# Retention layer: the values of two heads as seven products of halves, and the order of the layer's units rewritten

## The chip, the cores and the metric

The kernel runs on one core of one Trainium2 chip. A core has a matrix engine (TensorE; PE in the profile, with its weight loads as PEld), a vector engine (VectorE, DVE), an activation engine (ScalarE, ACT), a general engine (GpSimd, POOL) and a queue engine (SyncE, SP) that only issues transfers. Each engine carries out its own instructions strictly in the order in which the program issued them; engines wait for each other by semaphores. The metric is the device time of one execution in microseconds, the median over the runs shown. Times in rows of the trace are microseconds from the first instruction of the profiled execution.

## The reference

A trunk of two layers over 512 tokens of width 1024, all in float32. Layer 0 mixes tokens with a gated MLP, layer 1 with retention; each is followed by a squared-ReLU MLP (1024 to 4096 to 1024), and a last RMSNorm ends the trunk. The change lies in the retention layer:

```python
h = rmsnorm(x, norm_mix_g[1])
proj = h @ w_in                              # 1024 x 6144
q, k, v, g = split(proj, [1024, 2048, 4096]) # 4 heads: q, k 256 wide; v, g 512 wide
q, k = rotary(q), rotary(k)
for each head:                               # decay[i, j] = gamma ** (i - j) for i >= j
    o = ((q @ k.T) * decay) @ v
    o = rmsnorm(o, head_norm_g)              # over the 512 columns of the head
y = o * silu(g)
x = x + y @ w_out                            # 2048 x 1024
```

(The reference runs over chunks of 128 tokens with a state; over the 512 tokens of this input that is the formula above.)

## The kernel before

Everything is feature-major: `xT` holds the residual as 8 tiles of 128 features by 512 tokens. A float32 product is done as three fast products: each operand is split in a high part (a rounded copy, by ScalarE) and a low part (what the rounding left, by VectorE), and `mm3` (L263) issues high*high, high*low and low*high into one PSUM bank. So weights arrive in 1 MB blocks (`Raw`, 512 columns of a 512-row or 256 columns of a 1024-row slab), each is cut in two pieces of 128 x 1024 numbers (`Piece`), and each piece is split by one ScalarE copy (L222, tile wH) and one VectorE subtraction (L229, tile wL). A piece normally feeds 24 matmuls of 512 columns.

The program order is written out by hand. `step` records a unit of work with its pieces; a loop at the end (L1129) issues the units one after the other. A unit issues its matmuls and then, in this order, `advance()` (the next part of every unfinished evacuation), `refill()` and its hook `behind` (other work placed there). `refill` (L248) runs ahead: it issues the high part of the piece three units on and the low part of the piece two units on; after each low part `load_raws` (L185) issues every further weight load for which a place is free: two own buffers, a third (`extra`) where a stage has set one up, or a tile of the common pool of 16 8-KB buffers (`big`). A weight block that is the sum of two blocks of the matrix is loaded by SP, and the second block is then added by a transfer that POOL issues (L201, `accum_op=add`); that instruction waits on POOL until the first load has landed.

The second MLP matrix already runs through `seven` (L724): the 2x2 block product [activations: token halves by feature halves] x [weights: row halves by column halves] is formed from seven products of halves instead of eight (Strassen's scheme in Winograd's form). Products 1, 3, 4 and 5 use sums of activation blocks, which `make(s)` forms on VectorE (L753 to L760) and splits in high and low parts (L768, L769), one product ahead; each product takes two weight pieces that feed only 12 matmuls each; the results are added into a token-major tile from three running PSUM accumulators (L799 copy on ScalarE the first time, L801 add on VectorE afterwards). There the products alternate with units of the first MLP matrix (`up`).

The norm is applied late. `hH`, `hL` hold x*g split in two; the factor 1/rms per token is put on the results. `norm` (L344) computes it in four parts that hooks call one by one: split the sum of squares (ScalarE, POOL); two matmuls, a masked sum on VectorE and a power on POOL (L299, tile r4); split of that and two diagonal matrices on VectorE (L336, tile dg); two matmuls that spread it over the partitions and a copy to `rbc` (L342, tile wide).

The retention layer consists of these units of four pieces each (96 matmuls): `v_unit(h)` (values; scaled with r4 and split at evacuation, L920, L921), `qk_unit(h)` (queries and keys; rotary at evacuation with tables that carry rbc: L890 to L900), `g_unit(h)` (gates: z = psum*rbc on VectorE, L996; sigmoid on ScalarE, L997; z*sigmoid on VectorE, L999) and `o_unit(h)` (output projection). `scores(h, j)` and `av(h, c)` are small groups of matmuls that run in the hooks; `head_norm(h)` and `make_y(h, ..)` finish a head. The order before is v0, qk0, g0 (with the scores of head 0), qk1 (with av 0), v1 (scores 1, norm of head 0), g1 (av 1), o0 (norm 1), and then qk, v, g, o(h-1) for heads 2 and 3, and o3.

Of the kernel before, what the change touches and what calls it, by code (L numbers as in the profile page):

```python
# [10 lines left out]
F32 = mybir.dt.float32  # L11
# [77 lines left out]
def trunk(ctx, tc, x, norm_mix_g, norm_ffn_g, a_w_in, a_b_in, a_v_norm_g, a_w_s, a_b_s, a_w_out,  # L89
# [170 lines left out]
    def do(fn):  # L260
        step(lambda: fn())
# [461 lines left out]

    def seven(l, q):  # L724

        w = mlp_w2[l]

        def part(i, j):
            r, c = 1024 * q + 512 * i, 512 * j
            return w[r : r + 512, c : c + 512].rearrange("(k p) n -> p k n", p=P)  # L730
# [9 lines left out]
        def block(h, ts, c):  # L740
            return aF[2 * q + h][:, 2 * c : 2 * c + 2, ts]

# [3 lines left out]
        def make(s):  # L746

            def src(c):
                if s in (0, 2, 6):
                    return block(*((0, lo_t), None, (1, lo_t), None, None, None, (1, hi_t))[s], c)  # L750
                if s == 1:
                    sums["s", c] = half(tmp(f"sa{l}{q}{c}", "uz"))
                    nc.vector.tensor_sub(out=sums["s", c], in0=block(0, hi_t, c), in1=block(1, hi_t, c))  # L753
                elif s == 3:
                    nc.vector.tensor_sub(out=sums["s", c], in0=sums["s", c], in1=block(0, lo_t, c))
                elif s == 4:
                    nc.vector.tensor_add(out=sums["s", c], in0=sums["s", c], in1=block(1, lo_t, c))
                else:
                    sums["d", c] = half(tmp(f"sd{l}{q}{c}", "sq"))
# [4 lines left out]
            sp = parts[s] = big([P, 2, 4, T // 2], F32R, f"sp{l}{q}{s}")  # L764
            for c in range(2):
                v = src(c)
                hi, lo = sp[:, 0, 2 * c : 2 * c + 2, :], sp[:, 1, 2 * c : 2 * c + 2, :]
                nc.scalar.copy(out=hi, in_=v)  # L768
                nc.vector.tensor_sub(out=lo, in0=v, in1=f32(hi))  # L769
# [4 lines left out]

        PLAN = (0, 1, 2, 3, 5, 4, 6) if q == 2 else range(7)

        def one(s, i):
            after = dict(zip(PLAN, PLAN[1:])).get(s)

            def run(p):  # L780
                bk = BANK[s]
                if i == 0 and s in FIRST:
                    banks[bk] = [acc(f"sm{l}{q}{bk}{t}") for t in range(2)]
                sp = parts[s]
                for t in range(2):
                    ts = slice(t * P, (t + 1) * P)
                    for k in range(2):
                        kk = 2 * i + k
                        mm3(banks[bk][t], sp[:, 0, kk, ts], sp[:, 1, kk, ts], p.hi[:, k, :], p.lo[:, k, :], s in FIRST and kk == 0, kk == 3, True)
                advance()  # L790
                refill()
                if i == 0 and after is not None:
                    make(after)
                if i == 1:
                    (m, n), op = OUT[s]
                    for t in range(2):
                        v = tok[n][:, 2 * m + t, :]
                        if (n, m) in fresh:
                            nc.scalar.activation(v, banks[bk][t], AF.Copy, scale=1.0 if op == ALU.add else -1.0)  # L799
                        else:  # L800
                            nc.vector.tensor_tensor(out=v, in0=v, in1=banks[bk][t], op=op)  # L801
                    fresh.discard((n, m))
            return run

        return (lambda: make(0)), [lambda s=s: [step(one(s, i), pl[s][i]) for i in range(2)] for s in PLAN]

    fresh = set()

    def dense(l, hooks):
# [6 lines left out]
        for q in range(3):  # L816
            pl = pieces_f(mlp_w1[l], (0, D), (1024 * (q + 1), 1024 * (q + 2)))
            first, products = seven(l, q)
            do(first)
# [51 lines left out]
    nrm1 = norm("mix1")  # L871
    tab, qk, vv, pp, oo, gt = {}, {}, {}, {}, {}, {}
    POFF = [0, 512, 896, 1152]

    def load_b():
        tab["t"] = big([P, 4, T], F32, "trg")
        nc.sync.dma_start(out=tab["t"][:, 0:2, :], in_=trig)
        tab["d"] = big([P, H, T], F32, "dec")
        nc.sync.dma_start(out=tab["d"], in_=decay)

    def trig_scaled():
        for i in range(2):
            nc.vector.tensor_mul(tab["t"][:, 2 + i, :], tab["t"][:, i, :], rbc)

    def rope(h, which, pa, pb):
        cos, sin = tab["t"][:, 2, :], tab["t"][:, 3, :]
        if which == 0:
# [37 lines left out]
    def scores(h, j):  # L925
# [10 lines left out]
        def gen():  # L936
            pm = tmp(f"pm{h}{j}", "sq")
            hi, lo = pp[h][0][:, POFF[j] : POFF[j] + n], pp[h][1][:, POFF[j] : POFF[j] + n]
            nc.vector.tensor_mul(pm[:, :n], ps[:, :n], tab["d"][:, h, :n])
            nc.scalar.copy(out=hi, in_=pm[:, :n])  # L940
# [4 lines left out]
    def av(h, c):  # L945

        if c == 0:
            oo[h] = big([P, 4, T], F32, f"o{h}")
        vhi, vlo = vv[h]
# [7 lines left out]
        def gen():  # L957
# [8 lines left out]
            nc.scalar.activation(o, ps, AF.Copy, scale=gT[:, HG + 4 * h + c : HG + 4 * h + c + 1])  # L966
            yield
# [34 lines left out]
    def v_unit(h, behind=None):  # L1002
        tokens(pieces_t(bw, (0, D), (VW + h * DV, VW + (h + 1) * DV)), hs, evac_vv(h), f"vv{h}", behind)

    def g_unit(h, behind):
        pl = pieces_f(bw, (0, D), (GWT + h * DV, GWT + (h + 1) * DV))
        for i in range(4):
            feat(pl[i], hs, evac_g(h, i), f"g{h}_{i}", behind.get(i))

# [18 lines left out]
    hn0, sc1 = head_norm(0), each(scores, 1)  # L1028
    fin = {0: nxt(hn0), 1: nxt(hn0, 2), 2: lambda: (next(hn0, None), make_y(0, (0, 1))), 3: lambda: make_y(0, (2, 3))}
# [148 lines left out]
```

## Time and profile before

| | |
|---|---|
| median of 3 runs | 1372.65 us (1372.46 to 1373.21) |
| the profiled execution's own time | 1372.68 us |
| its span, first to last instruction | 1371.0 us |
| TensorE busy | 1360.9 us, 99% of the span |
| VectorE / ScalarE / POOL busy | 856.5 us (62%) / 566.7 us (41%) / 166.5 us (12%) |
| granted TensorE clock, mean | 0.998 |
| retention layer, first to last matmul | about 625.6 to 1025.4 us |

A matmul's row lasts about 0.39 us, though one starts every 0.227 us, as they are pipelined: 24 matmuls of 512 columns take 5.44 us. So the time of TensorE is counted in starts, and a bubble is seen as a hole between two starts. For the other engines the start-to-start distance of two instructions that wait for nothing is what one costs.

### The profile page before, as it was taken

The numbers are of one execution on the slowest core, as the hardware profiler recorded it, in microseconds if no ns is written. First come the engines' busy times: TensorE is split into PE (matmuls) and PEld (weight loads), VectorE is DVE, ScalarE is ACT, GpSimd is POOL, SyncE is SP. The second block draws the span as 40 slices with busy tenths as digits, with TensorE's granted clock in tenths as the row PEclk, the third lists the DMA queues.
The fourth block names the chain that finished last, engine by engine and source line by source line (L and its number), as shares of the span: only waits on it lengthen the run. The fifth ranks groups of instructions, "written<-read, shape, count | busy, mean of one in ns | idle before, by whom it ended". The sixth has DMA issues, their size and how long they took to land.

```text
span 1371.0 us, 15352 instructions
## 1 busy us (share of the span) xinstructions
PE 1360.9 (99%) x6184; PEld 1131.5 (83%) x6184; DVE 856.5 (62%) x1088; ACT 566.7 (41%) x812; POOL 166.5 (12%) x132
## 2 busy tenths in 40 slices
PE   9999999999999999999999999999999999999997
PEld 7888888888888888888888888888888888888886
DVE  7756756675666756775655574474594665665653
ACT  4646634334544434422333432333333543444342
POOL 4001111130100000021112110100121000100002
PEclk9999999999999999999999999999999999999999
DMA  6332222245674748322222222132127375674721
GB/s 233 126 104 92 67 87 93 93 133 153 154 206 126 212 126 184 124 102 94 80 75 78 76 92 93 62 115 70 62 93 213 92 185 160 155 207 126 174 85 61
DMA packets 115799, 166.70 MB, mean 122 GB/s; under 512 B 2880, under 2 KB 67984, under 8 KB 115472
## 3 DMA queue, kind: packets, MB, share of 16 engines
q1 hardware_dynamic: 102448, 139.50, 30.5%
q0 software_dynamic: 12672, 25.17, 10.8%
q8 instruction: 48, 0.79, 0.2%
q10 hardware_dynamic: 608, 1.06, 0.2%
q14 instruction: 23, 0.19, 0.0%
HBM read 163.62 MB, written 2.10 MB: 121 GB/s over the span
## 4 chain that ended last, share of the span: by engine, by line
PE 95%; DVE 2%; DMA 1%; issue 0%; ACT 0%; POOL 0%; SPq 0%; POOLq 0%; DVEq 0%; ACTq 0%
PE up L266 24%; PE g L266 6%; PE ro L266 6%; PE vv L266 6%; PE qk L266 6%; PE u L266 6%; PE o L266 6%; PE v L266 4%; PE dt L266 3%; PE dn L266 2%; PE av L266 2%; PE sm11a L266 2%; PE sm10a L266 2%; PE sm01a L266 2%; PE sm00a L266 2%; PE sm12a L266 2%
## 5 line engine op out<-in xcount | busy, mean ns | idle before, releaser
L229 DVE TENSOR_TENSOR wL<-raw,wH 128x1024 fp32r<-128x1024 f32 x235 | 300.3, 1282 | 49.9 <-issue 13.8
L222 ACT CAST wH<-raw 128x1024 fp32r<-128x1024 f32 x235 | 243.9, 1045 | 78.6 <-PE dt L266 12.8
L266 PE MATMUL up<-hH,wH 128*128 128x512 f32 x480 | 187.2, 390 | 0.2 <-ACT xtok L1047 0.2
L266 PE MATMUL up<-hL,wH 128*128 128x512 f32 x480 | 186.8, 389 | 0.0
L266 PE MATMUL up<-hH,wL 128*128 128x512 f32 x480 | 186.8, 389 | 0.0
L701 ACT ACTIVATE aF<-r 128x512 f32<-128x512 f32 x54 | 34.2, 633 | 218.2 <-DVE r L700 218.2
L700 DVE SCALAR_TENSOR_TENSOR r<-up,wide 128x512 f32<-128x512 f32 x54 | 37.4, 692 | 127.3 <-PE up L266 120.1
L266 PEld LDWEIGHTS up<-hH,wH 128*128 128x128 f32 x480 | 90.1, 188 | 19.0 <-ACT xtok L1047 0.5
L266 PEld LDWEIGHTS up<-hH,wL 128*128 128x128 f32 x480 | 90.1, 188 | 18.9
L266 PEld LDWEIGHTS up<-hL,wH 128*128 128x128 f32 x480 | 90.1, 188 | 18.7
L201 POOL DMA_DIRECT2D raw<-in_mlp_w_dram x22 | 28.6, 1298 | 390.4 <-DVE wL L229 244.6
L295 POOL TENSOR_TENSOR ssq<-ssq,sq 128x512 f32<-128x512 f32 x28 | 44.1, 1576 | 151.2 <-ACT sq L294 150.9
L229 DVE TENSOR_TENSOR wL<-more,wH 128x1024 fp32r<-128x1024 f32 x40 | 48.8, 1219 | 5.8 <-issue 4.4
L266 PE MATMUL u<-hH,wH 128*128 128x512 f32 x128 | 50.6, 395 | 0.0
L266 PE MATMUL g<-hH,wH 128*128 128x512 f32 x128 | 50.5, 395 | 0.0
L266 PE MATMUL o<-yH,wH 128*128 128x512 f32 x128 | 50.4, 394 | 0.0
L266 PE MATMUL qk<-hH,wH 128*128 128x512 f32 x128 | 50.0, 391 | 0.0
L266 PE MATMUL vv<-wH,hH 128*128 128x512 f32 x128 | 50.0, 391 | 0.0
L266 PE MATMUL ro<-ryH,wH 128*128 128x512 f32 x128 | 50.0, 390 | 0.0
L266 PE MATMUL ro<-ryH,wL 128*128 128x512 f32 x128 | 50.0, 390 | 0.0
L266 PE MATMUL ro<-ryL,wH 128*128 128x512 f32 x128 | 49.9, 390 | 0.0
L266 PE MATMUL vv<-wL,hH 128*128 128x512 f32 x128 | 49.9, 390 | 0.0
(369 smaller groups left out, 3069.5 us busy)
## 6 DMA issues: line engine op xcount, KB each, us to landing
raw<-in_mlp_w_dram SPq DMA_DIRECT2D x50, 1024.0 KB, 5.1
raw<-in_b_w_in_dram SPq DMA_DIRECT2D x24, 1024.0 KB, 4.9
raw<-in_mlp_w_dram POOLq DMA_DIRECT2D x22, 1024.0 KB, 8.6
more<-in_mlp_w_dram SPq DMA_DIRECT2D x20, 1024.0 KB, 5.2
raw<-in_a_w_in_dram SPq DMA_DIRECT2D x14, 1024.0 KB, 5.1
raw<-in_a_w_out_dram SPq DMA_DIRECT2D x8, 1024.0 KB, 4.9
raw<-in_b_w_out_dram SPq DMA_DIRECT2D x8, 1024.0 KB, 4.9
raw<-in_a_w_in_dram SPq DMA_DIRECT2D x8, 256.0 KB, 6.6
```

The costliest lines, as they stand in the source:

```text
L201: nc.gpsimd.dma_start(out=r.tile, in_=src, accum_op=ALU.add)
L222: nc.scalar.copy(out=p.hi, in_=p.src)
L229: nc.vector.tensor_sub(out=p.lo, in0=p.src, in1=f32(p.hi))
L266: nc.tensor.matmul(ps, lhsT=a, rhs=b, start=start and i == 0, stop=stop and i == 2, skip_group_check=resumed)
L295: nc.gpsimd.tensor_tensor(out=state["ssq"], in0=state["ssq"], in1=sq, op=ALU.add)
L700: nc.vector.scalar_tensor_tensor(out=r, in0=ps, scalar=0.0, in1=rbc, op0=ALU.max, op1=ALU.mult)
L701: nc.scalar.activation(a, r, AF.Square)
```

## The change

`seven` is generalised (any matrix, any activations, any destination) and now also forms the values of heads 0 and 1, which are one 512 x 1024 block of results:

- The layer begins with the gates of head 0 (pieces g0_0, g0_1, g0_2) instead of the values of head 0; the three later parts of the norm run in their hooks. After g0_2, `normed(0)` forms four tiles x*g*rbc in plain float32 (`hn[0]`, four VectorE instructions) and product 0's operand is split; then g0_3; then `normed(1)` (four more). The gates of head 0 wait in their PSUM banks until that is done (`"hn" in state`).
- Then the seven products, in the order 0, 1, 2, 3, 5, 4, 6, with the four gate pieces of head 1 (in the two other PSUM banks) behind the first four: p0 g1_0 p1 g1_1 p2 g1_2 p3 g1_3 p5 p4 p6. A third weight buffer (`morev`) is set up for this stage.
- The results land in `vF[0]`, `vF[1]` and are split in high and low parts later (`split_v`, 4 ScalarE copies and 4 VectorE subtractions for a head). They already carry 1/rms, so the scaling at evacuation is gone for these heads.
- The attention output of heads 0 and 1 is multiplied with gain and gate in one VectorE instruction straight from PSUM, in the gate's tile; before, it was a ScalarE copy with the gain and a later VectorE product.
- The tables of rotary and decay are loaded after the products, the rotary ones into small tiles, the decay ones for two heads at a time (`load_decay(2)` later), instead of ahead of the last MLP product of layer 0.
- The order of the rest is new: qk0; qk1 (scores 0 in its first two hooks, av 0 in its last two); v2 (scores 1, norm and y of head 0); o0 (av 1); qk2 (norm and y of head 1); o1 (scores 2); g2 (av 2); qk3 (norm and y of head 2); v3 (scores 3); g3 (av 3); o2 (norm and y of head 3); o3.

The core of the diff (in `seven` itself only names change; `plan` replaces `PLAN`):

```diff
-    def seven(l, q):
-        w = mlp_w2[l]
+    def seven(w, row, col, act, dst, name, plan=range(7)):
...
-            return aF[2 * q + h][:, 2 * c : 2 * c + 2, ts]
+            return act(h)[:, 2 * c : 2 * c + 2, ts]
...
-    do(lambda: (flush(), load_b()))
+    do(flush)
...
     def load_b():
-        tab["t"] = big([P, 4, T], F32, "trg")
-        nc.sync.dma_start(out=tab["t"][:, 0:2, :], in_=trig)
-        tab["d"] = big([P, H, T], F32, "dec")
-        nc.sync.dma_start(out=tab["d"], in_=decay)
+        tab["t"] = big([P, 4, T], F32, "tab")
+        tab["raw"] = [zt(f"trg{i}") for i in range(2)]
+        for i in range(2):
+            nc.sync.dma_start(out=tab["raw"][i], in_=trig[:, i, :])
+        load_decay(0)
...
+    def normed(c):
+        hn[c] = big([P, 4, T], F32, f"hn{c}")
+        for i in range(4):
+            k = 4 * c + i
+            nc.vector.scalar_tensor_tensor(out=hn[c][:, i, :], in0=xT[k], scalar=gT[:, MIX + 8 + k : MIX + 9 + k], in1=rbc, op0=ALU.mult, op1=ALU.mult)
+
+    def split_v(h):
+        vv[h] = [big([P, NT, DV], F32R, f"vv{n}{h}") for n in "HL"]
+        for n in range(NT):
+            nc.scalar.copy(out=vv[h][0][:, n, :], in_=vF[h][:, n, :])
+            nc.vector.tensor_sub(out=vv[h][1][:, n, :], in0=vF[h][:, n, :], in1=f32(vv[h][0][:, n, :]))
...
+            if h < 2:
+                nc.vector.scalar_tensor_tensor(out=o, in0=ps, scalar=gain, in1=o, op0=ALU.mult, op1=ALU.mult)
+                return
...
+            while "hn" not in state:
+                yield
...
-    v_unit(0, {0: nxt(nrm1), 1: nxt(nrm1, 2), 3: nxt(nrm1)})
-    do(trig_scaled)
-    qk_unit(0)
-    g_unit(0, each(scores, 0))
-    qk_unit(1, each(av, 0))
...
-    v_unit(1, {i: (lambda i=i: (sc1[i](), fin[i]())) for i in range(4)})
-    g_unit(1, each(av, 1))
-    o_unit(0, behind=finish_head(1))
-    for h in (2, 3):
-        qk_unit(h)
-        v_unit(h, each(scores, h))
-        g_unit(h, each(av, h))
-        o_unit(h - 1, behind=finish_head(h))
+    gs = g_pieces(0, {0: nxt(nrm1), 1: nxt(nrm1, 2), 2: nxt(nrm1)})
+    for p in gs[:3]:
+        p()
+    first, products = seven(bw, 0, VW, lambda h: hn[h], vF, "v", (0, 1, 2, 3, 5, 4, 6))
+    do(begin_values)
+    do(lambda: (normed(0), first()))
+    gs[3]()
+    do(lambda: (normed(1), state.update(hn=True)))
+    gs = g_pieces(1, banks=(mis,) * 4)
+    for i, p in enumerate(products):
+        p()
+        if i < 4:
+            gs[i]()
+    do(lambda: (extra.clear(), load_b()))
+    qk_unit(0, {0: trig_scaled, 2: lambda: split_v(0)})
+    sc, a = each(scores, 0), each(av, 0)
+    qk_unit(1, {0: both(sc[0], sc[1]), 1: both(sc[2], sc[3]), 2: both(a[0], a[1]), 3: both(a[2], a[3])})
+    hn0, sc = head_norm(0), each(scores, 1)
+    v_unit(2, {0: both(sc[0], sc[1], lambda: split_v(1), nxt(hn0)), 1: both(sc[2], sc[3], nxt(hn0, 2)),
+               2: both(nxt(hn0), lambda: make_y(0, (0, 1))), 3: lambda: make_y(0, (2, 3))})
+    do(lambda: load_decay(2))
+    o_unit(0, behind=each(av, 1))
+    hn1 = head_norm(1)
+    qk_unit(2, {0: nxt(hn1), 1: nxt(hn1, 2), 2: both(nxt(hn1), lambda: make_y(1, (0, 1))), 3: lambda: make_y(1, (2, 3))})
+    o_unit(1, behind=each(scores, 2))
+    g_unit(2, each(av, 2))
...
```

More of the change, by code (lines that the diff above doesn't have):

```diff
@@ L751, in src @@
                 if s == 1:
-                    sums["s", c] = half(tmp(f"sa{l}{q}{c}", "uz"))
+                    sums["s", c] = half(tmp(f"sa{name}{c}", "uz"))
                     nc.vector.tensor_sub(out=sums["s", c], in0=block(0, hi_t, c), in1=block(1, hi_t, c))
@@ L758, in src @@
                 else:
-                    sums["d", c] = half(tmp(f"sd{l}{q}{c}", "sq"))
+                    sums["d", c] = half(tmp(f"sd{name}{c}", "sq"))
                     nc.vector.tensor_sub(out=sums["d", c], in0=block(0, lo_t, c), in1=block(0, hi_t, c))
@@ L773, in seven @@
         OUT = [((0, 0), ALU.add), ((1, 1), ALU.add), ((0, 0), ALU.add), ((0, 1), ALU.subtract), ((0, 1), ALU.add), ((1, 1), ALU.subtract), ((1, 0), ALU.add)]
-        PLAN = (0, 1, 2, 3, 5, 4, 6) if q == 2 else range(7)
         def one(s, i):
-            after = dict(zip(PLAN, PLAN[1:])).get(s)
+            after = dict(zip(plan, plan[1:])).get(s)
             def run(p):
@@ L782, in run @@
                 if i == 0 and s in FIRST:
-                    banks[bk] = [acc(f"sm{l}{q}{bk}{t}") for t in range(2)]
+                    banks[bk] = [acc(f"sm{name}{bk}{t}") for t in range(2)]
                 sp = parts[s]
@@ L803, in one @@
             return run
-        return (lambda: make(0)), [lambda s=s: [step(one(s, i), pl[s][i]) for i in range(2)] for s in PLAN]
+        return (lambda: make(0)), [lambda s=s: [step(one(s, i), pl[s][i]) for i in range(2)] for s in plan]
     fresh = set()
@@ L817, in dense @@
             pl = pieces_f(mlp_w1[l], (0, D), (1024 * (q + 1), 1024 * (q + 2)))
-            first, products = seven(l, q)
+            first, products = seven(mlp_w2[l], 1024 * q, 0, lambda h, q=q: aF[2 * q + h], tok, f"{l}{q}", (0, 1, 2, 3, 5, 4, 6) if q == 2 else range(7))
             do(first)
@@ L947, in av @@
         if c == 0:
-            oo[h] = big([P, 4, T], F32, f"o{h}")
+            oo[h] = gt[h] if h < 2 else big([P, 4, T], F32, f"o{h}")
         vhi, vlo = vv[h]
@@ L1031, in trunk, with both, begin_values @@
-    g_unit(1, each(av, 1))
-    o_unit(0, behind=finish_head(1))
-    for h in (2, 3):
-        qk_unit(h)
-        v_unit(h, each(scores, h))
-        g_unit(h, each(av, h))
-        o_unit(h - 1, behind=finish_head(h))
+    def both(*fns):
+        return lambda: [f() for f in fns]
+    def begin_values():
+        extra.append(big([P, 2048], F32, "morev"))
+        fresh.update((n, m) for n in range(2) for m in range(2))
+        for n in range(2):
+            vF[n] = big([P, NT, DV], F32, f"vF{n}")
@@ L1038, in trunk @@
+    o_unit(1, behind=each(scores, 2))
+    g_unit(2, each(av, 2))
+    hn2 = head_norm(2)
+    qk_unit(3, {0: nxt(hn2), 1: nxt(hn2, 2), 2: both(nxt(hn2), lambda: make_y(2, (0, 1))), 3: lambda: make_y(2, (2, 3))})
+    v_unit(3, each(scores, 3))
+    g_unit(3, each(av, 3))
+    o_unit(2, behind=finish_head(3))
     o_unit(H - 1, gcol=FFN + 8)
```

28 lines of the change are left out of this document (16 added, 12 removed).

## The prediction

> **What bounds the kernel now.** I read the page first (busy shares, granted clock, the chain that ended last), then the chain in order of time, then windows by stage, and last the instruction rows of each engine around the places that change.
>
> ```profile
> span 1371.0 us, 15352 instructions
> PE 1360.9 (99%) x6184; PEld 1131.5 (83%) x6184; DVE 856.5 (62%) x1088; ACT 566.7 (41%) x812; POOL 166.5 (12%) x132
> PEclk9999999999999999999999999999999999999999
> PE 95%; DVE 2%; DMA 1%; issue 0%; ACT 0%; POOL 0%; SPq 0%; POOLq 0%; DVEq 0%; ACTq 0%
> ```
>
> TensorE is the bound: 95% of the chain, at full clock. The chain in order of time (start, length, line, count) shows what a unit costs:
>
> ```profile
> 338.30 5.44 PE sm00a L266 x24
> 625.63 10.94 PE vv L266 x48
> 637.05 10.93 PE vv L266 x48
> ```
>
> 24 matmuls take 5.44 us (0.227 each), in a value unit (vv) as in a product of halves (sm). Two windows (length, then busy time of PE, PEld, DVE, ACT, POOL) tell how much room the others have in the retention layer, and in a stage where products and MLP units alternate:
>
> ```profile
> 626.00:1025.00 399.00, 399.00 (x1842) 334.41 (x1841) 235.75 (x319) 136.95 (x198) 57.97 (x44) 1.00 0.26 85
> 338.00:571.00 233.00, 233.00 (x1030) 192.93 (x1029) 146.69 (x181) 102.88 (x136) 14.12 (x11) 1.00 0.64 167
> ```
>
> VectorE is busy 59% in the layer and 63% in the mixed stage, and TensorE has no hole in either. So the layer gains only what matmuls go, and loses each moment in which a weight or an operand comes late.
>
> **What it saves.** Values of two heads: 8 units of 24 matmuls now, 7 products of 24 after. Saved 24 x 0.227 = 5.44 us, 0.40% of the time. Nothing else leaves TensorE, and with no hole in the layer's window the new order can fill none. Whether the gain stays is decided by three places.
>
> **Place A: the norm's power sits behind a transfer on POOL.** In g0_1 `refill` runs before the hook. Its low part of g0_3 frees a buffer, so the loads of gates 1 and of product 1's weight sum go out on SP, and the adding transfer of that sum goes into POOL's queue. Only then does the hook put the power of the norm (L299) into the same queue. The trace has this pair once already, in the MLP of layer 0 (SP's loads, the second of the two being the sum's; POOL's adding transfer; the power; VectorE's scaled sums just before and the diagonals behind):
>
> ```profile
> 305.94 0.92 SPq L167 DMA_DIRECT2D raw<-in_mlp_w_dram  x2
> 312.00 0.17 DVE L327 TENSOR_SCALAR ms_ffn<-ms_ffn 128x4 f32<-128x4 f32 x1
> 313.91 1.49 POOL L201 DMA_DIRECT2D raw<-in_mlp_w_dram  x1 [10.78 <-DMA raw<-in_mlp_w_dram]
> 314.92 1.54 POOL L299 TENSOR_TENSOR r<-ms_ffn,mhalf 128x4 f32<-128x4 f32 x1
> 316.81 1.28 DVE L336 TENSOR_TENSOR dg_ffn<-ident,sp_ffn 128x512 fp32r<-128x512 f32 x2
> ```
>
> The power's input was there at 312.17, but it ran at 314.92, after the transfer that had waited for its load. That load was issued at 305.94 + 0.92 - 0.37 = 306.49, so 7.4 us pass from issue to POOL's instruction, 1.0 to the power, and 3.2 more (to 318.09) until the diagonals are done. There MLP units could run without rbc. In the layer, as it is now:
>
> ```profile
> 631.00 1.85 DVE L229 TENSOR_TENSOR wL<-raw,wH 128x1024 fp32r<-128x1024 f32 x1 [0.38 <-PE vv L266]
> 632.88 0.37 SPq L167 DMA_DIRECT2D raw<-in_b_w_in_dram  x1
> 636.88 0.40 PE L266 MATMUL vv<-wH,hH 128*128 128x512 f32 x1
> 638.78 1.03 POOL L299 TENSOR_TENSOR r<-ms_mix,mhalf 128x4 f32<-128x4 f32 x1 [7.01 <-DVE ms_mix L327]
> 640.15 1.29 DVE L336 TENSOR_TENSOR dg_mix<-ident,sp_mix 128x512 fp32r<-128x512 f32 x2
> 647.82 0.40 PE L340 MATMUL bc_mix<-dg_mix,onesr 128*128 128x512 f32 x1
> 648.50 0.59 ACT L342 COPY wide<-bc_mix 128x512 f32<-128x512 f32 x1 [4.87 <-PE bc_mix L341]
> ```
>
> The low part at 631.00 is that of the layer's fourth unit, which will be g0_3; the load behind it leaves at 632.88. After the change the sum's load follows 0.55 later, at 633.4; POOL's transfer goes at 640.85, the power at 641.85 instead of 638.78, the diagonals end at 645.0 instead of 641.44. The third unit starts at 636.88 and would end at 642.32; now the spreading matmuls come right behind it (before: one unit later, at 647.82, which hid all this). TensorE waits 645.0 - 642.3 = 2.7; with the shorter copy of the pair in the second MLP (7.1 from issue) 2.4. I take 2.5. Bounds: 0, if the diagonals come as now (641.44); and the slowest load:
>
> ```profile
> DMA to landing us min/median/max: 2.9/5.1/9.6
> ```
>
> 9.6 instead of 7.4 makes 4.7.
>
> **Place B: VectorE between rbc and product 1.** rbc used to be wanted by the evacuations only. Now product 0 needs x*g*rbc, and VectorE has to make that, the operands of products 0 and 1, and the four gates that waited, in its queue's order. The prices (start to start where nothing is waited for):
>
> ```profile
> 323.20 3.09 DVE L706 TENSOR_TENSOR aF<-aF,wide 128x512 f32<-128x512 f32 x5
> 502.15 1.22 DVE L229 TENSOR_TENSOR wL<-raw,wH 128x1024 fp32r<-128x1024 f32 x1
> 503.28 0.69 DVE L753 TENSOR_TENSOR sa<-aF,aF 128x512 f32<-128x512 f32 x1
> 504.65 0.69 DVE L769 TENSOR_TENSOR sp<-sa,sp 128x512 fp32r<-128x512 f32 x1 [0.69 <-ACT sp L768]
> 507.24 1.22 DVE L229 TENSOR_TENSOR wL<-raw,wH 128x1024 fp32r<-128x1024 f32 x1
> 508.38 1.28 DVE L801 TENSOR_TENSOR ytok<-ytok,sm02a 128x512 f32<-128x512 f32 x2
> 649.71 2.73 DVE L921 SCALAR_TENSOR_TENSOR vvL<-vv,r,vvH 128x512 fp32r<-128x512 f32 x4 [5.99 <-ACT vvH L920]
> 678.47 1.28 ACT L997 ACT_TABLE_LOAD   x1
> 679.76 0.63 ACT L997 ACTIVATE gs<-gz 128x512 f32<-128x512 f32 x1
> 680.43 0.69 DVE L999 TENSOR_TENSOR gt<-gz,gs 128x512 f32<-128x512 f32 x1 [1.25 <-ACT gs L997]
> ```
>
> A 512-wide product 0.60 (3.09 for five), a fused one 0.67 (2.73 for four), a weight's low part 1.14 (502.15 to 503.28), a pair of summed operands 3.96 (503.28 to 507.24, each low part behind its ScalarE copy). rbc is there 1.27 after the spread starts (647.82 to 649.09). From rbc VectorE runs: hn[0] 2.7; operand of product 0 about 1.5 (two low parts, the second behind its copy); low part of p0's second piece 1.14; hn[1] 2.7; four z 2.4; low part of g1_0 1.14. That is 11.6, or 12.9 after the spread. TensorE does the spread (0.48), g0_3 and p0 (10.88) and can start g1_0, whose third matmul wants the low part: at 11.8. It waits 1.1. Then VectorE: operands of product 1, 3.96 plus some 0.6 because ScalarE is behind (table load 1.28, four sigmoids, a weight); four gate products 2.4; only then the low part of p1's first piece, 1.14: together 8.1, done at 21.0 after the spread. p1's second matmul wants it at 0.5 + 16.3 + 1.1 + 0.2 = 18.1. It waits 2.9. Sum 4.0. Bounds: 2.5 (table loaded early, no latency between engines) and 5.5 (ScalarE 1.6 behind, 0.1 for each handing over).
>
> **Place C: products 5, 4 and 6 without a gate between.** Each takes two low parts, an operand and two adds on VectorE: 2.3 + 4.0 + 1.2 = 7.4 against 5.44 of TensorE. The cycles before, with gates, take 10.5 of 10.88 (z 0.6, wait for the sigmoid about 0.7, gate 0.6, three low parts 3.4, operand 4.0, adds 1.2). By these prices VectorE enters the last three one product ahead and just keeps it; the weights of p4's second half and of p6 come within 0.5 of the need. The nearest row, where two products and splits stand together in the MLP, is short by about as much (the window's VectorE, third of the busy times, has no idle moment):
>
> ```profile
> 571.00:578.30 7.30, 7.20 (x31) 5.46 (x30) 7.30 (x10) 5.78 (x10) 0.00 (x0) 1.00 0.00 1
> PEld sm02a L266 <- DVE wL L229: 0.4, 1, 0.4
> PEld sm02a L266 <- DVE sp L769: 0.4, 1, 0.4
> ```
>
> I take 0.5; bounds 0 and 3.5 (two excesses of 2.0 less the lead).
>
> **The rest in one go.** 12 of the 1 MB moves in the stage go in 60 us, about the rate of the mixed stage above (167 GB/s), through three buffers as there. The rotary tables go behind a weight load on SP and land some 7 us into qk0; the first table product waits for them on VectorE, and TensorE wants nothing from that before qk1. split_v (8 copies, 8 subtractions of 0.60), the adding copies of results and the fused gate (for a ScalarE copy and a product) lie beside 21.8 us units. In the new order y of heads 0 to 2 is finished in the last two hooks before its o unit, no longer a unit ahead: its last low parts end about 0.3 us before the third and fourth group of the first o piece want them, and scores 1 meet their keys with 0.1 to spare, since the fused gate keeps VectorE until the last av. I take 0.4; bounds -0.5 and 2.
>
> **Sum.** -5.44 + 2.5 + 4.0 + 0.5 + 0.4 = +2.0 us. The profiled execution took 1372.68 us (span 1371.0), 0.03 from the median of 1372.65; so about 1374.6.
>
> **The rivals.**
> 1. *The two waits are small and the gain stays.* Place A needs the sum's load early or the adding transfer behind the power, place B a VectorE that overlaps more than its rows of before. For it: the mixed stage has no hole with the same products. Against it: that stage has 8 units before its first product in which the late rbc is worked off; here there is one. With A at 0.5 and B at 1.5: -5.44 + 2.0 + 0.3 = -3.1, 1369.5; with nothing lost 1367.2.
> 2. *VectorE becomes the bound until the last product.* The place is C: if its cycle with a gate passes 10.88, that is if each of its two waits costs 0.2 more than here, no lead is left at p5, and the excess of 2.0 for each of p5 and p4 falls on TensorE: 1374.6 + 3.5 = 1378.1, slower. It decides from a lead of less than about 3 us at p5 on. For it: the window of the MLP's last products, 7.30 of 7.30 us. Against it: a lead of a whole product by my steps.
> 3. *A wait makes TensorE slow afterwards.* No row shows it: the clock row has full speed in every slice, and the longest wait is too short to tell. If one of the waits in A or B set the clock to half for 3.4 us, fifteen matmuls would each last 0.227 longer: 1374.6 + 3.4 = 1378. The Trainium skill ("TensorE: Matmul & The Clock Gate", section "What's actually happening") states just that: after an idle window of about 3.4 us the array runs at half clock. My longest wait, 2.9, would be under it; no run here shows it.
>
> **How the numbers follow.** My case 0.45, rival 1 0.22, rival 2 0.25, rival 3 0.06; 0.02 is left. 0.2% is 2.7 us (about what a measurement of this kernel tells from no change). My case spans 1372 to 1377 and is mostly within; faster comes from rival 1, slower from rivals 2 and 3 and the upper edge of mine. Faster 0.22, same 0.42, slower 0.36. The range takes in most of rivals 1 and 2: 1368.4 to 1379.
>
> **What would show it.** A: POOL's L299 right behind an L201 near 641, and TensorE idle before the spread (L340). B: matmuls of g and of the first piece of p1 waiting for DVE L229, about 1 and 3 us. C: holes in p4 and p6 of at most 0.5. Clock row at 9 throughout. If L299 runs before the first L201, or VectorE has its low parts ready, the time falls under 1370; holes from p5 on put it above 1377.

## The result and the profile after

The changed kernel takes 1391.74 us (median of 4 runs, 1391.5 to 1392.01), the kernel before 1372.61 beside it (4 runs, 1372.46 to 1373.21). The ratio is 1.0139, with a 95% interval of 1.0121 to 1.0156: slower by 19.1 us, where 24 matmuls went that had cost 5.44. The lines of its page that answer to those shown of before (busy time of each engine, the granted clock by slice, the chain that ended last):

```profile
span 1389.8 us, 15396 instructions
PE 1363.5 (98%) x6160; PEld 1130.2 (81%) x6160; DVE 887.4 (64%) x1130; ACT 579.4 (42%) x832; POOL 171.2 (12%) x136
PEclk9999999999999999999999999999999999999999
PE 39%; DVE 3%; POOL 1%; ACT 1%; issue 0%; POOLq 0%; ACTq 0%
```

Two subtractions give the whole balance. TensorE is idle for 1389.8 - 1363.5 = 26.3 us, before for 1371.0 - 1360.9 = 10.1: 16.2 more. And it is busy for 1363.5, though 1360.9 - 5.4 = 1355.5 were due: 8.0 more. 16.2 + 8.0 - 5.4 = 18.8, the difference of the spans. So there are waits, and the matmuls themselves became slower somewhere. (The shares of the chain don't add up to 100 here. I read the stages from the waits and the windows instead.)

The waits of TensorE's weight loads, by what ended them (total, count, longest; us; qkH and qkL are the high and low part of the rotated queries and keys, ryH and ryL those of y). The profile before has no hole over 0.25 us in the retention layer:

```profile
PEld sc L266 <- ACT qkH L915: 5.3, 2, 5.0
PEld bc_mix L340 <- issue: 3.7, 1, 3.7
PEld ro L266 <- ACT ryH L1004: 3.6, 2, 2.0
PEld smvc L266 <- DVE wL L229: 2.3, 2, 1.9
PEld sc L266 <- DVE qkL L916: 2.0, 3, 0.8
PEld st_h L321 <- issue: 1.3, 1, 1.3
```

bc_mix and smvc are the prediction's places A and B. sc (scores waiting for keys), ro (the o unit waiting for y) and st_h are not. Read from start to start of the matmuls, the holes over 0.25 us add to 17.8 us: 3.7 at the spread of the norm (place A), 1.6 at product 1 (place B), 0.8 at the first weighted sums, and 11.7 behind them: 2.0 at scores 1 and the norm of head 0 (0.58 and 1.40), 4.0 at the second o unit, 5.7 at the last head's scores. One of 0.2 lies at the second weight piece of product 4 (place C).

The slower matmuls don't show in the clock row, whose slices are 35 us long. Windows of 2 us (length; busy time of PE, PEld, DVE, ACT, POOL with counts; then the granted clock) and the matmuls behind place A show them:

```profile
648.00:650.00 2.00, 2.00 (x6) 1.56 (x5) 2.00 (x4) 0.62 (x1) 0.00 (x0) 0.50 1.10 202
652.00:654.00 2.00, 2.00 (x10) 1.64 (x10) 2.00 (x4) 1.03 (x1) 0.00 (x0) 1.00 0.19 16
860.00:862.00 2.00, 2.00 (x6) 1.52 (x6) 2.00 (x4) 0.00 (x0) 0.95 (x1) 0.50 0.52 183
948.00:950.00 2.00, 1.94 (x5) 1.56 (x6) 1.83 (x3) 1.05 (x2) 0.00 (x0) 0.50 0.00 0
```

```profile
647.25 0.58 PE L266 MATMUL g<-hH,wH 128*128 128x512 f32 x1
...
650.89 0.39 PE L266 MATMUL g<-hH,wH 128*128 128x512 f32 x1
651.12 0.39 PE L266 MATMUL g<-hL,wH 128*128 128x512 f32 x1
```

In the first window 6 matmuls fill 2 us, in the second 10. From 647.25 to 650.89 nine matmuls take 3.64 us, 0.40 each, where nine at 0.227 take 2.04: 1.6 lost. Then the full clock is back at once. There are three such stretches, behind the waits at the spread, at the second o unit and at scores 3, of 1.6, 1.6 and 1.5 (0.36 of the last counts among the holes above): 4.7 of the 8.0 us. The rows of matmuls that reach into the holes make some 1.3 more (0.39 long, where the next one follows after 0.227 otherwise). The last 2 are not traced.

**Place A** stands as predicted. POOL's queue, and the matmul that wants the diagonals (in brackets idle time of the engine before the instruction and what ended it):

```profile
642.18 1.30 POOL L201 DMA_DIRECT2D raw<-in_b_w_in_dram  x1 [10.52 <-DMA raw<-in_b_w_in_dram]
643.00 1.54 POOL L299 TENSOR_TENSOR r<-ms_mix,mhalf 128x4 f32<-128x4 f32 x1
```

```profile
645.71 0.47 PE L340 MATMUL bc_mix<-dg_mix,onesr 128*128 128x512 f32 x1 [3.29 <-DVE dg_mix L336]
```

**The second o unit** is where the order shows. VectorE's queue, then ScalarE's, and the matmuls that wait:

```profile
841.54 0.69 DVE L325 TENSOR_TENSOR own_h<-st_h,ident 128x512 f32<-128x512 f32 x1 [4.64 <-PE st_h L322]
...
844.51 0.16 DVE L313 TENSOR_TENSOR sp_h<-rh,sp_h 128x4 fp32r<-128x4 f32 x1 [1.36 <-ACT sp_h L312]
844.59 1.28 DVE L336 TENSOR_TENSOR dg_h<-ident,sp_h 128x512 fp32r<-128x512 f32 x2
845.79 0.68 DVE L906 TENSOR_TENSOR m<-qk,tab 128x512 f32<-128x512 f32 x1
...
849.73 1.94 DVE L916 TENSOR_TENSOR qkL<-m,qkH 128x512 fp32r<-128x512 f32 x2 [1.47 <-ACT qkH L915]
...
852.73 1.29 DVE L1003 TENSOR_TENSOR gt<-gt,wide 128x512 f32<-128x512 f32 x2
854.10 1.29 DVE L1006 TENSOR_TENSOR ryL<-gt,ryH 128x512 fp32r<-128x512 f32 x2
```

```profile
851.81 0.57 ACT L342 COPY wide<-bc_h 128x512 f32<-128x512 f32 x1
853.45 1.22 ACT L1004 CAST ryH<-gt 128x512 fp32r<-128x512 f32 x2 [1.07 <-DVE gt L1003]
```

```profile
854.12 0.50 PE L266 MATMUL ro<-ryH,wH 128*128 128x512 f32 x1 [1.16 <-ACT ryH L1004]
857.83 0.50 PE L266 MATMUL ro<-ryH,wH 128*128 128x512 f32 x1 [1.55 <-ACT ryH L1004]
```

Three chains share the engines' queues in the hooks of this query and key unit: the head's norm (sums, POOL's power, diagonals, ScalarE's copy of the spread L342, y), the rotary (four products, POOL's two adds, ScalarE's copy, VectorE's low part) and the low parts of weights. Each goes to POOL or ScalarE and back, and what comes behind it in VectorE's queue waits for the way back. VectorE stands idle for 4.64 us until the sums come, and then everything is wanted at once; 1.36 more are idle on the power's way. The query's two banks are full when the sums are (the norm's spread of sums is the next thing on TensorE), but the rotary's first product goes at 845.79, behind six instructions of the norm. Its low parts wait 1.47 for POOL and ScalarE, and y, behind them, a weight and the copy of the spread, arrives 1.3 us after TensorE wants it; its second half, 1.7 after.

**The last head's scores** repeat this one round further on. The chain in order of time (start, length, instruction):

```profile
934.23 0.63 ACT qkH L915
935.58 1.14 DVE wL L229
...
938.00 1.29 DVE ryL L1006 x2
...
941.73 1.29 DVE ryL L1006 x2
943.02 0.60 DVE m L906
944.96 1.27 POOL m L910
946.26 0.63 ACT qkH L915
948.06 2.07 PE sc L266 x4
```

The keys' rotary (943.02) is queued behind y of head 2, which TensorE wants only two units later. Scores 3 want its keys now, and wait 5.7 us.

### The profile page after: what moved, and what is told of

Read it like the earlier page. It is cut to its first block, busy times and chain, and to the rows that moved or that the text cites. A ratio compares the mean times of both kernels' runs of the same rounds, so it can differ in the third digit from the quotient of the medians.

```text
span 1389.8 us, 15396 instructions
## 1 busy us (share of the span) xinstructions
PE 1363.5 (98%) x6160; PEld 1130.2 (81%) x6160; DVE 887.4 (64%) x1130; ACT 579.4 (42%) x832; POOL 171.2 (12%) x136
## 5 line engine op out<-in xcount | busy, mean ns | idle before, releaser
L266 PEld LDWEIGHTS up<-hH,wL 128*128 128x128 f32 x480 | 90.1, 188 | 18.8
L266 PE MATMUL g<-hL,wH 128*128 128x512 f32 x128 | 50.7, 396 | 0.0
L266 PE MATMUL g<-hH,wL 128*128 128x512 f32 x128 | 50.5, 395 | 0.0
```

The source lines that it names most:

```text
L266: nc.tensor.matmul(ps, lhsT=a, rhs=b, start=start and i == 0, stop=stop and i == 2, skip_group_check=resumed)
```

## The experiments

The times stand against a median of before from the same chip: 1372.67 for the first four, 1372.84 for the next four, 1372.97 for the last two.

**The order alone.** Only the new order is kept; the values of heads 0 and 1 come from ordinary units of 24 matmuls, the same values by another way.

```diff
-    first, products = seven(bw, 0, VW, lambda h: hn[h], vF, "v", (0, 1, 2, 3, 5, 4, 6))
...
+    plain_v(0)
+    g_unit(1, {})
+    plain_v(1)
```

> The new order with ordinary products: the values of heads 0 and 1 by 8 units of 24 matmuls in the place of the seven products (gates 1 between), scaled into the same float32 tiles and split later as in the changed kernel. Theory of the queues: what the order costs is still there; the matmuls saved (5.4) come back, the waits of the products' stage (3.5 + 1.6, and 1.7 of half clock) go: 1391.7 + 5.4 - 6.8 = 1390.3. Rival, the seven products make the loss: about 1372.7.

Measured 1388.48 (1388.3 to 1388.77), ratio 1.0115, interval 1.01 to 1.013: 15.8 us slower than before without one product of halves. The waits that lie behind the products are there as in the kernel after, those at A, at B and at the weighted sums are gone; the span and the two largest:

```profile
span 1386.9 us, 15358 instructions
PEld sc L266 <- ACT qkH L915: 6.0, 3, 5.0
PEld ro L266 <- ACT ryH L1004: 3.6, 2, 2.0
```

Its holes add to 12.9 us, the first starts of the slow stretch behind scores 3 among them, and the rest of that stretch to some 1.7; about 1.2 is not traced. So of the 19.1 us the order takes 15.8 (with what else changed around the products: the fused gate, the late splitting of the values, the later tables), and the seven products add 3.3 to it: they save 5.4 and lose 7.7 at A with its slow stretch (5.3), at B (1.6) and at the weighted sums (0.8). The other 1.0 is not worked out in full: the second o unit has a slow stretch in the one kernel and not in the other, which waits 1.05 at scores 2 in its place.

**The norms moved off the query and key units.** Norm and y of heads 1 and 2 go into the hooks of the gate and of the value unit, where no rotary runs.

```diff
-    qk_unit(2, {0: nxt(hn1), 1: nxt(hn1, 2), 2: both(nxt(hn1), lambda: make_y(1, (0, 1))), 3: lambda: make_y(1, (2, 3))})
+    g_unit(2, {0: nxt(hn1), 1: nxt(hn1, 2), 2: both(nxt(hn1), lambda: make_y(1, (0, 1))), 3: lambda: make_y(1, (2, 3))})
+    qk_unit(2)
     o_unit(1, behind=each(scores, 2))
-    g_unit(2, each(av, 2))
-    hn2 = head_norm(2)
-    qk_unit(3, {0: nxt(hn2), 1: nxt(hn2, 2), 2: both(nxt(hn2), lambda: make_y(2, (0, 1))), 3: lambda: make_y(2, (2, 3))})
-    v_unit(3, each(scores, 3))
+    qk_unit(3, each(av, 2))
+    hn2, sc = head_norm(2), each(scores, 3)
+    v_unit(3, {0: both(sc[0], nxt(hn2)), 1: both(sc[1], nxt(hn2, 2)),
+               2: both(sc[2], nxt(hn2), lambda: make_y(2, (0, 1))), 3: both(sc[3], lambda: make_y(2, (2, 3)))})
```

> The changed kernel, with the norm and y of heads 1 and 2 moved out of the hooks of the query-key units: head 1's beside the gates of head 2 (placed ahead of qk2), av 2 beside qk3, head 2's norm beside the values of head 3 with scores 3. Theory of the queues: norm and rotary of the same unit stand in one another's way in the orders of VectorE, POOL and ScalarE, and the o unit of head 1 (holes of 4.0 us) and scores 3 (5.7 us) wait for the end of that; with the two stretches of half clock behind (1.7 each) 13.1 us go: 1378.6. Rival, VectorE is full in this half of the layer: the holes come back in other places, above 1387.

Measured 1377.79 (1377.38 to 1378.09), ratio 1.0037, interval 1.0024 to 1.005: 14.0 us come back by this alone. The windows of the second o unit (here from 874.4 on, as the gates of head 2 went ahead of it) and of the last scores are full, at the full clock (after, the second of these windows is busy for 40.00 of its 45 us at a clock of 0.96; that row stands with the filled wait, below):

```profile
874.00:900.00 26.00, 26.00 (x124) 21.88 (x122) 14.74 (x21) 6.58 (x9) 2.54 (x2) 1.00 0.17 57
915.00:960.00 45.00, 45.00 (x214) 37.99 (x213) 26.91 (x40) 18.85 (x31) 12.78 (x9) 1.00 0.21 71
```

So both places, with their slow stretches, go with this edit. For the second o unit it leaves a rival, since it also makes y of head 1 a whole unit earlier: y might be late merely because it is made in the unit just ahead. Head 0 in the changed kernel speaks against that. Its norm and y stand in the last hooks of a value unit, just ahead of the first o unit, and TensorE has no hole there (it starts at 800.53). VectorE's queue of the changed kernel, at the head's sums and at the low parts of y's first half:

```profile
789.32 0.69 DVE L325 TENSOR_TENSOR own_h<-st_h,ident 128x512 f32<-128x512 f32 x1 [0.68 <-PE st_h L322]
797.24 1.29 DVE L1006 TENSOR_TENSOR ryL<-gt,ryH 128x512 fp32r<-128x512 f32 x2
```

That way takes 9.2 us (789.32 to 798.53). For head 1, with the rotary in the same hooks, it takes 13.9 (841.54 to 855.39), and the o unit follows its sums at the same distance. So the rotary between the norm and y makes the difference; for the last scores the next run shows it.

**The rotary first, for head 3.** Its products are issued ahead of the hook and the norm stays where it was.

```diff
             refill()
+            if ahead:
+                launch(evac(ps))
             if behind:
                 behind()
-            launch(evac(ps))
+            if not ahead:
+                launch(evac(ps))
```

> The changed kernel with one edit in the query-key unit of head 3: each piece issues its rotary before its hook (parts of head 2's norm and y) instead of behind it. Theory of the queues: the keys of head 3 are late because their rotary stands behind two weight parts and the whole of y in VectorE's order; in front of it they are ready before scores 3 want them, so the hole of 5.7 us and the 1.7 us of half clock go, while y of head 2 is wanted only two units later: 1391.7 - 7.4 = 1384.3. Head 1's hole (4.0) stays. Rival, VectorE simply has too much to do in these 30 us, in whatever order: the hole stays within 1.5 us, 1390 or more.

Measured 1387.52 (1387.36 to 1388.52), ratio 1.011, interval 1.0095 to 1.0126: 4.4 us gained where 7.4 were expected. The hole at scores 3 falls from 5.7 to 1.7 (1.43 and 0.24) and its slow stretch is gone, so the queue's order is the cause there. It doesn't go to nothing because the rotary of the last bank still meets y: VectorE's two products of y take 3.17 us while POOL runs its two adds from 939.70 on (1.29 where it doesn't), and ScalarE's copy of the keys stands in its queue behind that of y. VectorE's and POOL's rows:

```profile
933.96 1.29 DVE L1006 TENSOR_TENSOR o<-o,wide 128x512 f32<-128x512 f32 x2
940.07 3.17 DVE L1006 TENSOR_TENSOR o<-o,wide 128x512 f32<-128x512 f32 x2
```

```profile
939.70 1.28 POOL L913 TENSOR_TENSOR m<-m,m 128x512 f32<-128x512 f32 x1 [9.63 <-DVE m L911]
```

Other losses moved too: at the second o unit the same four waits had no slow stretch in this kernel, and TensorE, quicker there, then waits 1.1 us for the keys of scores 2, which it had not done.

**The adding transfer behind the power.** The transfer is held back by one hook and issued by `release`, so that POOL's queue has the power first.

```diff
-                nc.gpsimd.dma_start(out=r.tile, in_=src, accum_op=ALU.add)
+                if "held" in state:
+                    state["held"].append((r.tile, src))
+                else:
+                    nc.gpsimd.dma_start(out=r.tile, in_=src, accum_op=ALU.add)
...
-    gs = g_pieces(0, {0: nxt(nrm1), 1: nxt(nrm1, 2), 2: nxt(nrm1)})
+    gs = g_pieces(0, {0: both(nxt(nrm1), lambda: state.update(held=[])), 1: both(nxt(nrm1, 2), release), 2: nxt(nrm1)})
```

> The changed kernel, with one edit: the adding transfer of product 1's weights is issued on POOL behind the power of the norm instead of ahead of it. Its load leaves as before. If the power's place in POOL's queue makes the wait ahead of the spread (3.5 us in the changed kernel's trace) and the 3.4 us of half clock behind it (nine matmuls, 1.7 us), both go, but the wait at product 1 (1.6 us) grows by up to what the slow g0_3 gave VectorE in time: about 1391.7 - 5.2 + 1.7 = 1388.2. If the spread waits for something else: 1391.7.

Measured 1389.43 (1388.89 to 1390.39), ratio 1.0122, interval 1.0107 to 1.0137: 2.4 gained where 3.5 were expected. The hole at the spread is gone, which shows its cause. But place B now appears whole, first at the gate and then at product 1 (matmuls of this kernel that wait for a low part, and the clock behind them):

```profile
654.93 0.50 PE L269 MATMUL g<-hH,wL 128*128 128x512 f32 x1 [0.76 <-DVE wL L232]
662.43 0.50 PE L269 MATMUL smvc<-wL,spv 128*128 128x512 f32 x1 [1.97 <-DVE wL L232]
```

```profile
664.00:666.00 2.00, 2.00 (x6) 1.52 (x6) 1.25 (x3) 1.80 (x3) 1.09 (x1) 0.50 0.14 14
```

From start to start that is 0.93 + 2.13 = 3.1 us, and a slow stretch behind the second. In the kernel after, the wait and the slow stretch at A had given VectorE the time to get ahead: there it was 1.6. So the slow stretch at A wasn't lost whole in the kernel after, as VectorE was behind there anyway.

**The wait filled with matmuls.** Ahead of scores 3 TensorE runs 20 matmuls that nobody reads, some 4.5 us, as long as the wait.

```diff
+    def fill(n):
+        ps = mis("fill")
+        for _ in range(n):
+            nc.tensor.matmul(ps, lhsT=onesr, rhs=hH[0], start=True, stop=True)
...
-    v_unit(3, each(scores, 3))
+    v_unit(3, {0: both(lambda: fill(20), sc[0]), 1: sc[1], 2: sc[2], 3: sc[3]})
```

> The changed kernel with 20 matmuls of 512 columns (4.5 us, into a bank that nobody reads) ahead of the first scores of head 3, where TensorE waits 4.8 us for the keys. If the wait itself sets the clock to half for the 3.4 us behind it, the filled wait keeps the clock at full speed and the time falls by 1.7 us to 1390.0, with the scores issued at the same moment. If the slow matmuls have another cause, or the filler delays the scores, 1391.7 or more.

Measured 1390.45 (1389.92 to 1390.81), ratio 1.0128, interval 1.0111 to 1.0145. The clock stays at full speed here, where after it fell to half (the same window of this kernel, then of the kernel after):

```profile
915.00:960.00 45.00, 44.58 (x195) 35.97 (x194) 29.31 (x39) 15.24 (x23) 9.05 (x7) 1.00 0.23 75
```

```profile
915.00:960.00 45.00, 40.00 (x169) 32.38 (x168) 29.34 (x39) 14.76 (x22) 8.80 (x7) 0.96 0.22 71
```

Against its before the kernel is 17.8 us slower, after 19.1; the intervals of the two ratios overlap, and the second o unit has no slow stretch in this kernel either, so it is the clock that decides here and not the time. Two other kernels that leave a wait of 4.8 us open at this place (the order alone, and the transfer behind the power) have a clock of 0.92 in this window. With the wait filled the slow stretch is gone: it comes from TensorE's own idleness. Its price is read from the starts of the matmuls, 1.5 us here in the kernel after, 1.6 at place A.

**The mends together.** The transfer behind the power, the norms moved, and of the four waiting gates only two are evacuated ahead of product 1's operand:

```diff
-            while "hn" not in state:
+            while h == 0 and state.get("hn", 0) < (1 if c < 2 else 2):
...
+        if i == 1:
+            do(lambda: state.update(hn=2))
```

> Three edits together: the add behind the power, the norms of heads 1 and 2 off the query-key units, and only two of the four waiting gates of head 0 evacuated ahead of product 1 (the other two behind it). From the run with the norms moved (1377.8): the wait ahead of the spread and its half clock go (3.8 + 1.7); the wait ahead of product 1 is 3.1 us once the spread is in time, and four VectorE products of 0.60 fewer stand ahead of it: 0.7 left instead of 1.7. Sum 1377.8 - 5.5 - 1.0 = 1371.3, about 1.3 faster than the kernel before. If VectorE makes up for it at products 5, 4, 6: 1373 or more.

Measured 1371.66 (1371.33 to 1372.14, 11 runs), ratio 0.9992, interval 0.9983 to 1.0001. Left are holes of 0.83 at product 1, 0.77 at the weighted sums, 0.59 at scores and 1.41 at the norm of head 0. Two more edits take one each:

```diff
-                nc.vector.scalar_tensor_tensor(out=o, in0=ps, scalar=gain, in1=o, op0=ALU.mult, op1=ALU.mult)
+                og = z2t(f"og{h}{c}")
+                nc.scalar.activation(og, ps, AF.Copy, scale=gain)
+                yield
+                nc.vector.tensor_mul(o, og, o)
```

> As the run before this one, and the attention output of heads 0 and 1 evacuated as in the kernel before the change: a ScalarE copy with the gain and a later VectorE product, instead of one VectorE instruction that waits for TensorE. If that instruction holds up VectorE's queue between qk1 and v2, the three holes there (0.8, 0.6, 1.4) shrink: 1371.3 - 1.5 = 1369.8. If they come from split_v and the two scores in one hook, they stay, and the extra instructions cost nothing: 1371.3.

Measured 1371.14 (1370.44 to 1372.3), ratio 0.9988, interval 0.9979 to 0.9996: only the hole at scores went. The other edit splits the values of head 1 in two halves over two hooks, so that the decay products (pm) of the scores don't stand behind all eight instructions:

```diff
-    v_unit(2, {0: both(sc[0], sc[1], lambda: split_v(1), nxt(hn0)), 1: both(sc[2], sc[3], nxt(hn0, 2)),
+    v_unit(2, {0: both(sc[0], sc[1], nxt(hn0), lambda: split_v(1, (0, 1))), 1: both(sc[2], sc[3], nxt(hn0, 2), lambda: split_v(1, (2, 3))),
```

> As the run with the three edits, and the split of head 1's values taken apart: two of its four parts in v2's first hook behind the start of the norm, two in the second. If the hole of 1.4 us ahead of head 0's norm matmuls (they wait for a bank that VectorE reads last) comes from split_v standing ahead in VectorE's queue, it goes: 1371.3 - 1.4 = 1369.9. If the fused gate is the cause: 1371.3.

Measured 1370.82 (1370.48 to 1371.28), ratio 0.9985, interval 0.9976 to 0.9994; the hole of 1.41 is 0.35.

**The mended order with ordinary values** tells what the products themselves are worth (the order of the last kernel, the value units of the first experiment).

```diff
+    plain_v(0)
+    g_unit(1, {})
+    plain_v(1)
...
+    g_unit(2, {0: nxt(hn1), 1: nxt(hn1, 2), 2: both(nxt(hn1), lambda: make_y(1, (0, 1))), 3: lambda: make_y(1, (2, 3))})
+    qk_unit(2)
```

> The mended order (norms and y off the query and key units, splitting in two halves) with ordinary value units of 24 matmuls in the place of the seven products, so with no adding transfer and no gate that waits. Theory: the order's loss is mended whole and the products are worth 5.44 less the two holes of 0.8 that they still have (first weight of product 1, the weighted sums behind it), so here TensorE has the time before plus the two small holes at scores (about 0.6 + 0.35): 1373.7, some 2.9 above the same order with the products (1370.82). Rival: the products save nothing by themselves and what is gained comes from the order: 1370.8 here too, or lower.

Measured 1374.17 (1373.87 to 1374.65), ratio 1.001, interval 1.0001 to 1.0019: 1.2 us above before. The same order with the products is 2.0 below before (1370.82 against 1372.84). So they are worth 3.2 of their 5.4 us; holes of 0.82 and 0.78 take 1.6, the other 0.6 I haven't traced. And no order tried here gains anything by itself.

**All mends**: the kernel with the values split in halves, and the fused product undone as above.

```diff
+                og = z2t(f"og{h}{c}")
+                nc.scalar.activation(og, ps, AF.Copy, scale=gain)
```

> All mends together: power ahead of the adding transfer, norms off the query and key units, half of the waiting gates later, splitting in two halves, and the evacuation of the weighted sums by ScalarE with the gate's product later. Theory: the holes left are product 1's (0.8) and that of the weighted sums (0.8), since the one at scores (0.57) went when the fused product was undone: 1370.82 - 0.6 = 1370.2. Rival: ScalarE's extra copies come in the way of the first halves and the hole only moves: 1370.8 or more.

Measured 1370.12 (1369.62 to 1371.53, 11 runs), ratio 0.998, interval 0.9971 to 0.9989: the lowest median, 2.9 us below before (its interval overlaps that of the kernel with the values split in halves). Its span, its busy times and the two largest waits left in the layer:

```profile
span 1367.9 us, 15417 instructions
PE 1356.5 (99%) x6160; PEld 1127.4 (82%) x6160; DVE 886.6 (65%) x1130; ACT 584.2 (43%) x840; POOL 173.1 (13%) x136
PEld smvc L269 <- DVE wL L232: 1.5, 2, 1.1
PEld av L269 <- DVE pL L962: 0.8, 1, 0.8
```

Idle time is 11.4 (before 10.1, after 26.3), busy time 1.0 above the 1355.5 that were due.

## Why the prediction was wrong

1374.6 was predicted and 1391.74 came; the range ended at 1379. Slower by 2.0 was forecast, and slower by 19.1 it is: the three places that were worked out cost nearly what they were priced at, and the order, priced at 0.4, made the loss.

- **What it saves**: 24 matmuls went, as counted. With the order mended, 3.2 of the 5.4 us arrive.
- **Place A**: the mechanism right, the size short. The load left as foreseen, but the transfer went at 642.18 instead of 640.85 and the wait was 3.7 instead of 2.5, within its bounds; with the slow stretch behind it, which was given a chance of 0.06, it was about 5.3.
- **Place B**: the mechanism right, the size within its bounds where nothing disturbs it. 1.1 and 2.9 were predicted, 0.93 and 2.13 stand in the kernel that mends A. In the kernel after it is 1.6 instead of 4.0, because TensorE was held up at A.
- **Place C**: 0.5 was said and 0.2 came, at the second weight piece of product 4, where the prediction had it. The second rival, VectorE as the bound there, didn't come. That A, B and C with the slow stretch at A cost 7.1 together, where 7.0 stood in the sum, is luck: the slow stretch was not in the sum, and what it and A took too much, B and C took too little.
- **The step that failed is "The rest in one go"**: 0.4 us, bounds -0.5 and 2, for everything that the new order does. It was worth 15.8. Three things went wrong in it. "Its last low parts end about 0.3 us before the third and fourth group of the first o piece want them" is said of heads 0 to 2 alike. It came true for head 0, whose y stands in the hooks of a value unit: no hole. Head 1's stands in those of a query and key unit, and there the rotary's way is not in the price: the way from the sums to y takes 13.9 us instead of 9.2, and TensorE waits 4.0. (For head 2 the sentence misreads the order: two units stand between its y and its o unit.) The keys of scores 3, queued behind y of head 2, and the norm of head 0 are not priced at all: 5.7 and 1.4. And scores 1 were to meet their keys with 0.1 to spare and waited 0.58. What the step left out at the two large places is the way back: the norm and the rotary both go from VectorE over POOL and ScalarE and return, and what stands behind them in VectorE's queue waits, as its idle 1.36 and 1.47 in the middle of that stretch show. Places A and B were worked out as queues, instruction by instruction; for the hooks of the query and key units no such working stands in the prediction.
- **The first rival** (small waits, 1369.5) is near the mended kernel (1370.1), not the changed one.
- **The third rival** (a wait makes TensorE slow): true, three times. Its price was mis-sized, 3.4 us instead of 1.5 to 1.6: fifteen matmuls fill 3.4 us at the full clock, but at half only eight go into it, and nine took 3.64. One of the three places is A, as the rival had it, behind a wait of 3.7 us.
- **Slower** had 0.36. The mark set in the prediction, "holes from p5 on put it above 1377", pointed to the last products. The large holes were ahead of them and behind them.

## What to carry to other kernels

An order that moves an engine's work from one unit to another is priced queue by queue, like a wait: write down for each engine what stands behind which instruction, and count the way to the other engines and back, not busy time. In this kernel two chains that both leave VectorE and return did not fit into the hooks of one unit: count whether the unit has time for both, one after the other. Where a change has two parts, measure each alone before judging either: here the products were sound and the order around them spent five times their worth.

## What the runs showed of the hardware

- A wait of TensorE has an aftermath. After the waits of 3.7 and 4.8 us the granted clock fell to 0.50, behind the first of them for 3.6 us, with the matmuls 0.40 us apart on average (0.43 in the middle) instead of 0.227: a loss of 1.6 us. The loss varies: 1.5 us behind the 4.8 us in the kernel after, 2.7 behind the same wait in the kernel with the order alone.
- How long a wait has to be isn't fixed. A wait of 2.13 us was followed by half clock in the kernel with the transfer behind the power, and one of 2.15, at the same matmul, was not in the kernel with the rotary first. The four waits at the second o unit (1.32, 0.49, 1.72, 0.50) were followed by it in the kernel after, at the clock shown above, and not in four others that have them too (the order alone, the transfer behind the power, the wait filled, the rotary first). This is the last of them:

```profile
856.00:862.00 6.00, 4.23 (x17) 2.92 (x16) 5.92 (x10) 1.68 (x3) 0.10 (x1) 1.00 0.54 175
```

The Trainium skill ("TensorE: Matmul & The Clock Gate", section "What's actually happening") says that activity is judged over windows of about 3.4 us that run on freely, whatever the kernel does. The unlike outcomes of like waits agree with it: by it, how much of a wait falls into one window would decide, and the kernel doesn't choose that. No run here shows where a window begins. That a whole idle window is needed, as that section states, is more than these runs bear out, since 2.13 us are no such window.
- Some of VectorE's products slow down beside POOL's: two that took 1.29 us took 3.17 while POOL ran two adds of the same size. These read two tiles in SBUF, the on-chip memory of the tiles. So does the product of output and gate in the kernel before, which took 1.73 instead of 0.68 the three times that POOL worked on tiles of the same size beside it. The rotary's products, which read a PSUM bank and a tile, kept their 0.68 beside POOL's adds (the last of four, at 847.59 in the kernel after).
